# Down projection: the streamed weight pieces issued from ScalarE, and the fourth chain of weight sums in idle gate tiles

## The chip, the cores and the metric

The kernel runs on one core of one Trainium2 chip. The metric is the device time of one execution in microseconds (us). The kernel before takes 1087.72 us, the median of three runs (1086.67 to 1089.07). All data is float32.

## The reference

One block of a network on 512 tokens with 1024 features: a gated convolution branch and a state-space branch, mixed and added to `x`, and then a feed-forward part. The change touches only the last lines of this (with `FFN_HIDDEN` = 2816):

```python
    x = x + rms_norm(mixed, mix_post_g[i])
    h = rms_norm(x, ffn_pre_g[i])
    gt, up = jnp.split(h @ w_gate_up[i], 2, axis=-1)
    f = (jax.nn.silu(gt) * up) @ w_down[i]
    x = x + rms_norm(f, ffn_post_g[i])
```

The product `@ w_down` is the **down projection**: 512 tokens x 2816 features times 2816 x 1024 weights. `h @ w_gate_up` just ahead of it is the **gate/up stage**.

## The kernel before, in words

**Split numbers.** TensorE (PE) multiplies a reduced-precision float32 type. Every operand is therefore kept as two tiles, a high part `hi` (a ScalarE copy that rounds) and a low part `lo` (VectorE: source minus `hi`), and each product is three matmuls, hi x hi, hi x lo and lo x hi (`mm3`, lines 171 to 173). In this text a ScalarE copy is a *cast* and the VectorE subtraction a *sub*.

**The down projection.** Of the 22 blocks of 128 features, 16 go through a Strassen-Winograd scheme. The weights of these 16 blocks are cut into four quarters S11, S12, S21, S22; each quarter is stored as four pieces of 128 x 1024 numbers, 512 KB. Seven products replace eight, and each has four *jobs*, one for each piece j = 0 to 3, so there are 28 jobs of 12 matmuls. This document numbers them in the order in which they run:

| product | jobs | weights of job j | activations |
|---|---|---|---|
| p1 | 0 to 3 | S11 | `f32` as it is |
| p5 | 4 to 7 | S11 + S12 | a difference, made by VectorE |
| p6 | 8 to 11 | S11 + S12 + S22 | two sums, made by VectorE |
| p3 | 12 to 15 | S22 | a difference |
| p7 | 16 to 19 | S12 + S22 | a sum already there |
| p2 | 20 to 23 | S21 | as it is |
| p4 | 24 to 27 | S11 + S12 + S22 + S21 | as it is |

(Signs are put into the activations.) The other six feature blocks follow as plain products, "d".

**The chain.** The weights of p1, p5, p6 and p4 are made in place in one tile for each j, `chain0` to `chain3`. SyncE (SP) reads S11 into it; after the cast and the sub of p1, GpSimd (POOL) issues a DMA that reads S12 and *adds* it to the tile in memory (`chain_add`, line 1074); after those of p5 it adds S22 in the same way; in p2 VectorE adds S21 (line 1093). `chain0` to `chain2` (`NCE` = 3) have tiles of their own, read four steps before the end of the gate/up stage. For `chain3` there is no room then. Its S11 is read twice: once early into a streaming buffer, for job 3 alone (`raw_read("p1", NCE)`), and once into `chain3` in the pool `pf`, which takes the space of the gate/up stage and so can be filled only when that stage has ended (line 1030, called after `h2.close()`).

**The streamed pieces.** The weights of p3, p7 and p2, twelve pieces, pass through five rotating buffers (tag `raw`); each is read by a DMA that SP issues (`raw_read`, line 1069), and for p7 a POOL DMA adds S22 to it (line 1071). The same buffers serve the gate/up weights before and the plain products' weights after. A read waits for the last reader of its buffer, which is the sub of the piece five places earlier.

**Order.** Python code traces the instructions; a scheduler then orders each engine's stream by dependences, buffers and its own estimate of time, so an engine's order is not simply that of the code. Each engine then runs its stream in order, and an instruction whose input isn't there holds up all that stand behind it. `tc.keep_in_program_order(i)` pins `i` behind the instruction traced just before it on the same engine, without waiting for that one's result. `prepare(n)` is called ahead of job n: it traces the forms (activations, `f_form`, lines 1109 to 1122; weights, `w_form`, lines 1087 and 1088) up to job n + `S_AHEAD` = n + 4, and then the reads up to job n + `R_AHEAD` = n + 7.

**The gate tiles.** `second(u)` and `third(u)` of the gate/up stage keep the activated gate of a step in two 128 x 512 tiles, tags `sg0` and `sg1`, two buffers each, in the pool `h2e` (line 982). Only even steps take a new pair; step 20 takes the last. The other pair is last read by `third(19)` (lines 1017 and 1019).

Of the kernel before, what the change touches and what calls it, by code (L numbers as in the profile page):

```python
# [10 lines left out]
F32 = mybir.dt.float32  # L11
# [3 lines left out]
ALU = mybir.AluOpType  # L15
# [3 lines left out]
P = 128  # L19
T = 512  # L20
# [58 lines left out]
NPAIR = 8  # L79
NCE = 3  # L80
NQ = NPAIR // 2
S_AHEAD = 4
R_AHEAD = 7
BLOCKS = ("s11", "s12", "s21", "s22")

TAPS_GLU = 12
# [28 lines left out]
def block_kernel(ctx: ExitStack, tc: tile.TileContext, x, xT, prm, hp, gp, w, out):  # L115
# [863 lines left out]
    fp = ctx.enter_context(tc.tile_pool(name="f", bufs=1, side="right"))  # L979
    f32 = fp.tile([P, NF, T], F32, name="f32")  # L980
    ce = ctx.enter_context(tc.tile_pool(name="ce", bufs=1, side="right"))
    h2e = h2.enter_context(tc.tile_pool(name="h2e", bufs=2, side="right"))
    sg = {}
    c1, c2 = slice(0, HB), slice(HB, T)

# [39 lines left out]
    def piece_of(b, j):  # L1025
        return w[seq[(b, j)]]

    def chain_read(j, pool_):
        chain[j] = pool_.tile([P, 1024], F32, name=f"chain{j}")
        tc.keep_in_program_order(nc.sync.dma_start(chain[j], piece_of("s11", j)))  # L1030

    prev = None
    for u in range(NF):
        if u == NF - 4:
            for j in range(NCE):
                chain_read(j, ce)
        prep_s(u)
        prep_a(u + 1)
        prep_s(u + 1)
        if u >= EARLY_U:  # L1040
            first(u)
        if prev is not None:
            third(u - 1, prev)
        prev = second(u)
# [17 lines left out]

    def raw_read(p, j):
        key = (p, j)
        if key in read or (p in ("p5", "p6", "p4")) or (p == "p1" and j < NCE) or p == "d":
            return
        b = {"p1": "s11", "p3": "s22", "p7": "s12", "p2": "s21"}[p]
        t = read[key] = wp.tile([P, 1024], F32, tag="raw", bufs=RAW_BUFS, name=f"raw_{p}_{j}")
        tc.keep_in_program_order(nc.sync.dma_start(t, piece_of(b, j)))
        if p == "p7":  # L1070
            pool.dma_start(t, piece_of("s22", j), accum_op=ALU.add)

    def chain_add(b, j):
        pool.dma_start(chain[j], piece_of(b, j), accum_op=ALU.add)

    def w_form(n):
        p, j = jobs[n]
        if n in w_forms:
            return
        if p == "d":  # L1080
            w_split(seq[("wd", j)])
            w_forms[n] = split[seq[("wd", j)]]
            return
        raw_read(p, j)
        src = read[p, j] if (p, j) in read else chain[j]
        hi, lo = w_forms[n] = w_room(n)
        act.copy(hi, src)
        dve.tensor_tensor(out=lo, in0=src, in1=hi.bitcast(F32), op=ALU.subtract)
        follow = {"p1": "s12", "p5": "s22"}.get(p)
        if follow and (p, j) not in read:  # L1090
            chain_add(follow, j)
        if p == "p2":
            dve.tensor_tensor(out=chain[j], in0=chain[j], in1=src, op=ALU.add)

    def f_form(n):
        p, j = jobs[n]
# [27 lines left out]
    f_form(0)  # L1124
    for j in range(2):
        w_form(j)
    raw_read("p1", NCE)
    third(NF - 1, h2_last)
    h2.close()
    pf = ctx.enter_context(tc.tile_pool(name="pf", bufs=1))  # L1130
    room["pf"] = pf
    gpost1 = pf.tile([P, D], F32, name="gpost1")
    for j in range(NCE, NQ):
        chain_read(j, pf)
    nc.scalar.dma_start(gpost1, gp[1].partition_broadcast(P))
    room["s"] = pf.tile([P, NPAIR, HB], F32, name="s")
    ev = {(n, r): pf.tile([P, T], F32, name=f"ev{n}{r}") for n in ("p1", "p5", "p6", "mg") for r in range(2)}
    banks = {}

    def acc(name, r):  # L1140
# [16 lines left out]
    for n, (p, j) in enumerate(jobs[: NQ * len(PRODUCTS)]):  # L1157
        if n == 0:
            for m in range(2, NQ):
                w_form(m)  # L1160
            for m in range(NCE, NQ):
                chain_add("s12", m)
        prepare(n)
        name = dict(PRODUCTS)[p]
        (fh, fl), (wh, wl) = f_forms[p, j // 2], w_forms[n]
        for e in range(2):
            c, k = slice(e * T, (e + 1) * T), 2 * (j % 2) + e
            for r in range(2):
                tok = slice(r * P, (r + 1) * P)
                step(name, r, fh[:, k, tok], fl[:, k, tok], wh[:, c], wl[:, c], j == NQ - 1 and e == 1)  # L1170
        if j == NQ - 1:
            for r in range(2):
                if p in ("p1", "p5", "p6"):
                    act.copy(ev[p, r], banks[name, r])
                elif p == "p7":
                    dve.tensor_tensor(out=ev["p5", r], in0=banks[name, r], in1=ev["p5", r], op=ALU.add)
            if p == "p7":
                x2 = f32[:, :NPAIR, :].rearrange("p (t n) d -> p t (n d)", t=NT)
                tc.keep_in_program_order(nc.sync.dma_start(x2, x2d.rearrange("(t p) d -> p t d", p=P)))
# [25 lines left out]
    for t in range(NT):  # L1205
        i, r = t % 2, t // 2
        mg, sq = {}, {}
        for n in (1, 0):
# [2 lines left out]
            b_ = banks[NAME[i, n], r]  # L1211
            if (i, n) == (1, 0):
                sq[n] = mean_sq(b_, pf, f"c{t}", n)
                mg[n] = ev["mg", r]
            else:
                mg[n] = ev[{(0, 0): "p1", (0, 1): "p6", (1, 1): "p5"}[i, n], r]
                dve.tensor_tensor(out=mg[n], in0=b_, in1=mg[n], op=ALU.add if (i, n) == (0, 1) else ALU.subtract)
                sq[n] = mean_sq(mg[n], pf, f"c{t}", n)
                b_ = mg[n]
# [84 lines left out]
```

## Time and profile before

| | us |
|---|---|
| median of three runs | 1087.72 |
| the profiled execution, its own time | 1088.74 |
| its span (first to last instruction) | 1087.0 |
| gate/up stage's last matmul, p1's first matmul at | 960.36 |
| plain products run to about | 1080 |

All times of day in this document are microseconds from the span's start. A timeline row gives start, duration, engine, line, operation, output<-inputs, and in brackets how long the engine stood idle just before and what released it. "PEq", "SPq", "ACTq" are an engine's DMA issues. A row ending in "x2" is two instructions of one kind merged, from the first's start to the last's end. In a table of windows each engine's column is busy time and, in brackets, instructions; PEclk is the clock granted to TensorE, and the DMA share is that of the core's 16 DMA engines. A releaser is inferred: with two candidates the row shows the later one.

### The profile page before, as it was taken

What the parts mean: (1) busy time and instruction counts of PE and PEld (TensorE: products, weight loads), DVE (VectorE), ACT (ScalarE), POOL (GpSimd) and SP (SyncE); (2) the same over time, 40 slices, a digit from 0 to 9 for tenths busy, and PEclk for the clock granted to TensorE, in tenths of its full rate; (3) what the DMA queues carried; (4) which work ended last, traced back from release to release, by engine and by line L of the source; (5) the groups of instructions that cost most, each with busy time, mean ns of one, the idle gap of its engine ahead of it and who ended that gap; (6) DMA issues with size and microseconds to landing.
All of it is one profiled execution on the core that took longest, in us unless ns stands there. A gap on an engine that the chain in (4) does not pass through costs nothing.

```text
span 1087.0 us, 15652 instructions
## 1 busy us (share of the span) xinstructions
PE 1055.5 (97%) x6145; PEld 926.7 (85%) x6145; DVE 827.8 (76%) x1175; ACT 603.4 (56%) x968; POOL 89.3 (8%) x113
## 2 busy tenths in 40 slices
PE   8999999999999999999999999999999999997997
PEld 6888888988897889879888788878999999985886
DVE  6799995996698769697894455579988788658675
ACT  6657848586748464924223762466554554536541
POOL 2002001111111111100000000010000000011000
PEclk9999999999999999999999999999999999998999
DMA  7466643646535553452133222423343243166912
GB/s 280 126 175 208 153 120 98 175 117 194 136 98 142 160 138 102 117 136 78 39 97 117 78 97 78 174 97 117 116 137 98 85 159 126 26 185 147 287 53 78
DMA packets 38954, 139.80 MB, mean 129 GB/s; under 512 B 4576, under 2 KB 4832, under 8 KB 37856
## 3 DMA queue, kind: packets, MB, share of 16 engines
q1 hardware_dynamic: 28896, 99.93, 27.9%
q0 software_dynamic: 7776, 32.51, 14.5%
q10 hardware_dynamic: 2208, 6.36, 1.7%
q8 instruction: 48, 0.79, 0.3%
q14 instruction: 26, 0.21, 0.1%
HBM read 134.52 MB, written 4.26 MB: 128 GB/s over the span
## 4 chain that ended last, share of the span: by engine, by line
PE 76%; DVE 11%; ACT 3%; DMA 3%; issue 2%; POOL 1%; DVEq 0%; POOLq 0%; ACTq 0%; SPq 0%
PE xy L171 4%; PE xy L172 3%; PE xy L173 3%; PE pso L171 3%; PE pso L173 3%; PE pso L172 3%; PE yd L558 2%; PE px L173 2%; PE px L171 2%; PE px L172 2%; PE pz L171 2%; PE pz L172 2%; PE pz L173 2%; DMA raw<-in_w 2%; DVE a L398 2%
## 5 line engine op out<-in xcount | busy, mean ns | idle before, releaser
L138 ACT CAST whi<-raw 128x1024 fp32r<-128x1024 f32 (+1 forms) x118 | 120.8, 1032 | 213.9 <-PE pC L172 37.9
L398 DVE SCALAR_TENSOR_TENSOR a<-v,prm_t,a 128x485 f32<-128x485 f32 (+16 forms) x240 | 182.0, 762 | 4.2 <-ACT a L395 1.4
L143 DVE TENSOR_TENSOR wlo<-raw,whi 128x1024 fp32r<-128x1024 f32 (+1 forms) x84 | 99.7, 1194 | 46.4 <-ACT whi L138 46.3
L171 PE MATMUL pz<-whi,hhi 128*128 128x256 f32 (+1 forms) x256 | 73.6, 287 | 0.8 <-DVE sg L424 0.8
L172 PE MATMUL pz<-wlo,hhi 128*128 128x256 f32 (+1 forms) x256 | 72.2, 282 | 0.0
L173 PE MATMUL pz<-whi,hlo 128*128 128x256 f32 (+1 forms) x256 | 71.9, 281 | 0.0
L829 DVE TENSOR_TENSOR wlo_g<-raw,whi_g 128x1024 fp32r<-128x1024 f32 x40 | 48.2, 1220 | 10.1 <-ACT whi_g L828 10.1
L828 ACT CAST whi_g<-raw 128x1024 fp32r<-128x1024 f32 x40 | 40.9, 1048 | 23.9 <-issue 9.8
L141 POOL DMA_DIRECT2D wlo<-in_w x34 | 30.3, 892 | 274.8 <-ACT wlo L140 163.9
L171 PE MATMUL pso<-yh,whi 128*128 128x512 f32 x128 | 50.5, 396 | 0.6 <-DVE B L475 0.6
L173 PE MATMUL px<-hhi,wlo 128*128 128x512 f32 x128 | 50.4, 394 | 0.0
L172 PE MATMUL px<-hlo,whi 128*128 128x512 f32 x128 | 50.3, 393 | 0.0
L171 PE MATMUL px<-hhi,whi 128*128 128x512 f32 x128 | 50.2, 392 | 0.0
L173 PE MATMUL pso<-yh,wlo 128*128 128x512 f32 x128 | 50.2, 392 | 0.0
L172 PE MATMUL pso<-yl,whi 128*128 128x512 f32 x128 | 50.0, 391 | 0.0
L171 PEld LDWEIGHTS pz<-whi,hhi 128*128 128x128 f32 x256 | 48.3, 189 | 1.3 <-DVE sg L424 1.0
L172 PEld LDWEIGHTS pz<-wlo,hhi 128*128 128x128 f32 x256 | 48.1, 188 | 0.3
L173 PEld LDWEIGHTS pz<-whi,hlo 128*128 128x128 f32 x256 | 48.2, 188 | 0.2
L381 ACT ACTIVATE L<-L,nacs 128x128 f32<-128x128 f32 x128 | 41.4, 392 | 5.8 <-POOL L L375 5.6
L593 DVE TENSOR_SCALAR y<-y,rs 128x256 f32<-128x256 f32 x32 | 9.4, 349 | 36.2 <-POOL rs L179 36.2
L140 ACT ACTIVATE wlo<-whi 128x1024 fp32r<-128x1024 f32 x34 | 35.9, 1055 | 0.2
L475 DVE SCALAR_TENSOR_TENSOR x<-px,prm_t,x 128x511 f32<-128x511 f32 (+2 forms) x48 | 35.3, 743 | 0.5 <-ACT x L473 0.3
(512 smaller groups left out, 3388.7 us busy)
## 6 DMA issues: line engine op xcount, KB each, us to landing
raw<-in_w SPq DMA_DIRECT2D x161, 512.0 KB, 3.7
wlo<-in_w POOLq DMA_DIRECT2D x34, 512.0 KB, 5.3
L<-scr POOLq DMA_DIRECT2D x8, 1024.0 KB, 5.4
raw_p<-in_w SPq DMA_DIRECT2D x13, 512.0 KB, 9.0
chain<-in_w POOLq DMA_DIRECT2D x8, 512.0 KB, 8.5
xT<-in_xT SPq DMA_DIRECT2D x8, 256.0 KB, 5.6
xr<-in_x ACTq DMA_DIRECT2D x4, 512.0 KB, 4.9
x2d<-xr ACTq DMA_DIRECT2D x4, 512.0 KB, 2.6
```

The lines of the kernel that those rows point to most:

```text
L138: act.copy(hi[:, c], src[:, c])
L140: act.activation(lo[:, c], hi[:, c].bitcast(F32), AF.Copy, scale=-1.0)
L141: pool.dma_start(lo[:, c], w[n][:, c].bitcast(F32R), accum_op=ALU.add)
L143: dve.tensor_tensor(out=lo[:, c], in0=src[:, c], in1=hi[:, c].bitcast(F32), op=ALU.subtract)
L171: mark["pe"] = pe.matmul(ps, lh, rh, start=start, stop=False, skip_group_check=more)
L172: pe.matmul(ps, lh, rl, start=False, stop=False, skip_group_check=more)
L173: pe.matmul(ps, ll, rh, start=False, stop=stop, skip_group_check=more)
L381: act.activation(L[:, h, c, :], L[:, h, c, :], AF.Exp, bias=nacs[:, c, HG * g + h : HG * g + h + 1])
L398: return dve.scalar_tensor_tensor(out=va[j][:, d:], in0=vs[j][:, : T - d], scalar=col("dw_w", j * KC + KC - 1 - d), in1=va[j][:, d:], op0= ...
L475: dve.scalar_tensor_tensor(out=a[:, d:], in0=ps[:, : T - d], scalar=col("ssm_w", i * KS + KS - 1 - d), in1=a[:, d:], op0=ALU.mult, op1=ALU ...
L828: a_ = act.copy(hi, src)
L829: d_ = dve.tensor_tensor(out=lo, in0=src, in1=hi.bitcast(F32), op=ALU.subtract)
```

## The change

1. **Streaming reads.** The twelve reads of p3, p7 and p2 are issued by ScalarE (ACT) in place of SP, pinned in program order: each behind the ACT instruction traced just before it. With `R_AHEAD` = 8 that is the cast of job m-4 for the read of job m: the read for job 12 stands behind the cast of job 8, the read for job 16 behind the cast of job 12, and so on.
2. **The fourth place of the chain.** `chain3` is now two 128 x 512 halves in the idle pair of gate tiles, read by SP in the last step of the gate/up stage (`u == NF - 1`). The separate read of S11 for job 3 goes away. Job 3's, 7's, 11's and 27's casts and subs, both POOL additions and p2's VectorE addition are done by halves. The S12 addition to `chain3` now follows job 3's form, as for the other places.
3. **Space.** `h2e` is kept to the end of the kernel; `pf` loses `chain3` and the two `evmg` tiles, for which two idle 128 x 512 slices of `f32` are used.

```diff
-R_AHEAD = 7
+R_AHEAD = 8
...
-    h2e = h2.enter_context(tc.tile_pool(name="h2e", bufs=2, side="right"))
+    h2e = ctx.enter_context(tc.tile_pool(name="h2e", bufs=2, side="right"))
...
-    def chain_read(j, pool_):
-        chain[j] = pool_.tile([P, 1024], F32, name=f"chain{j}")
-        tc.keep_in_program_order(nc.sync.dma_start(chain[j], piece_of("s11", j)))
+    def chain_read(j):
+        if j < NCE:
+            chain[j] = [(ce.tile([P, 1024], F32, name=f"chain{j}"), slice(0, 1024))]
+        else:
+            chain[j] = [
+                (h2e.tile([P, T], F32, tag=f"sg{i}", bufs=2, name=f"chain{j}_{i}"), slice(i * T, (i + 1) * T))
+                for i in range(2)
+            ]
+        for t, c in chain[j]:
+            tc.keep_in_program_order(nc.sync.dma_start(t, piece_of("s11", j)[:, c]))
...
-                chain_read(j, ce)
+                chain_read(j)
+        if u == NF - 1:
+            chain_read(NCE)
...
-        if key in read or (p in ("p5", "p6", "p4")) or (p == "p1" and j < NCE) or p == "d":
+        if key in read or p not in ("p3", "p7", "p2"):
             return
-        b = {"p1": "s11", "p3": "s22", "p7": "s12", "p2": "s21"}[p]
+        b = {"p3": "s22", "p7": "s12", "p2": "s21"}[p]
         t = read[key] = wp.tile([P, 1024], F32, tag="raw", bufs=RAW_BUFS, name=f"raw_{p}_{j}")
-        tc.keep_in_program_order(nc.sync.dma_start(t, piece_of(b, j)))
+        tc.keep_in_program_order(nc.scalar.dma_start(t, piece_of(b, j)))
         if p == "p7":
             pool.dma_start(t, piece_of("s22", j), accum_op=ALU.add)
 
     def chain_add(b, j):
-        pool.dma_start(chain[j], piece_of(b, j), accum_op=ALU.add)
+        for t, c in chain[j]:
+            pool.dma_start(t, piece_of(b, j)[:, c], accum_op=ALU.add)
...
-        src = read[p, j] if (p, j) in read else chain[j]
         hi, lo = w_forms[n] = w_room(n)
-        act.copy(hi, src)
-        dve.tensor_tensor(out=lo, in0=src, in1=hi.bitcast(F32), op=ALU.subtract)
-        follow = {"p1": "s12", "p5": "s22"}.get(p)
-        if follow and (p, j) not in read:
-            chain_add(follow, j)
+        for src, c in [(read[p, j], slice(0, 1024))] if (p, j) in read else chain[j]:
+            act.copy(hi[:, c], src)
+            dve.tensor_tensor(out=lo[:, c], in0=src, in1=hi[:, c].bitcast(F32), op=ALU.subtract)
+        if p in ("p1", "p5"):
+            chain_add({"p1": "s12", "p5": "s22"}[p], j)
         if p == "p2":
-            dve.tensor_tensor(out=chain[j], in0=chain[j], in1=src, op=ALU.add)
+            for t, c in chain[j]:
+                dve.tensor_tensor(out=t, in0=t, in1=read[p, j][:, c], op=ALU.add)
...
-    raw_read("p1", NCE)
...
-    for j in range(NCE, NQ):
-        chain_read(j, pf)
...
-    ev = {(n, r): pf.tile([P, T], F32, name=f"ev{n}{r}") for n in ("p1", "p5", "p6", "mg") for r in range(2)}
+    ev = {(n, r): pf.tile([P, T], F32, name=f"ev{n}{r}") for n in ("p1", "p5", "p6") for r in range(2)}
...
-            for m in range(NCE, NQ):
-                chain_add("s12", m)
...
-                mg[n] = ev["mg", r]
+                mg[n] = f32[:, NPAIR + r, :]
```

## The prediction

> **What bounds the kernel now.** The page first: PE is busy nearly all the span, so only a stage where PE stands still can give much.
>
> ```profile
> span 1087.0 us, 15652 instructions
> PE 1055.5 (97%) x6145; PEld 926.7 (85%) x6145; DVE 827.8 (76%) x1175; ACT 603.4 (56%) x968; POOL 89.3 (8%) x113
> ```
>
> Then the table of windows over the down projection, cut where PE's timeline changes pace:
>
> ```profile
> 961.90:972.80 10.90, 10.90 (x50) 9.02 (x49) 8.93 (x8) 5.56 (x6) 2.86 (x4) 1.00 0.89 266
> 972.80:984.45 11.65, 10.13 (x42) 7.45 (x41) 4.61 (x4) 3.53 (x5) 2.29 (x3) 1.00 1.07 268
> 984.45:990.68 6.23, 0.00 (x1) 0.00 (x0) 3.72 (x5) 4.04 (x5) 0.87 (x1) 0.74 1.05 209
> 990.68:994.41 3.73, 3.69 (x8) 2.48 (x9) 3.73 (x4) 3.73 (x5) 0.00 (x0) 0.52 0.08 14
> ```
>
> PE stands still for 6.23 us, and then runs at a granted clock of 0.52. PE's timeline gives the size of the whole:
>
> ```profile
> 960.36 0.40 PE L171 MATMUL sx<-whi_s,whi_g 128*128 128x512 f32 x1
> ...
> 971.27 0.39 PE L171 MATMUL sv<-phi_s,fh 128*128 128x512 f32 x1
> ...
> 980.36 0.50 PE L171 MATMUL sv<-whi_s,fh 128*128 128x512 f32 x1 [0.76 <-ACT whi_s L1087]
> 981.62 0.50 PE L172 MATMUL sv<-wlo_s,fh 128*128 128x512 f32 x1 [0.76 <-DVE wlo_s L1088]
> ...
> 990.68 0.79 PE L171 MATMUL sx<-whi_s,fh 128*128 128x512 f32 x1 [6.23 <-ACT fh L1118]
> ...
> 994.48 0.40 PE L173 MATMUL sx<-whi_s,fl 128*128 128x512 f32 x1
> ```
>
> p1's 48 matmuls take 971.27 - 960.36 = 10.91 us, 0.2273 each. At that pace p6 (job 8) would start at 960.36 + 96 x 0.2273 = 982.18, and its ninth matmul, the one at 994.48, at 984.00. So the stage has lost **10.48 us** there: 2.1 in p5 (job 7), 6.4 waiting for p6's first activation `fh` (together 8.50), 1.98 to the slow clock after the stand.
>
> Why `fh` is late is in ACT's timeline, whose releasers are the additions to the chain:
>
> ```profile
> 961.83 0.36 ACTq L1135 DMA_DIRECT2D gpost<-in_gp  x1
> ...
> 972.21 1.05 ACT L1087 CAST phi_s<-chain 128x1024 fp32r<-128x1024 f32 x1 [4.26 <-DMA chain<-in_w]
> 979.26 1.05 ACT L1087 CAST whi_s<-chain 128x1024 fp32r<-128x1024 f32 x1 [5.99 <-DMA chain<-in_w]
> ...
> 982.35 1.05 ACT L1087 CAST whi_s<-chain 128x1024 fp32r<-128x1024 f32 x1 [1.07 <-DMA chain<-in_w]
> ...
> 987.69 1.04 ACT L1087 CAST whi_s<-chain 128x1024 fp32r<-128x1024 f32 x1 [1.47 <-DMA chain<-in_w]
> 988.64 1.04 ACT L1087 CAST whi_s<-raw_p 128x1024 fp32r<-128x1024 f32 x1
> 989.58 1.05 ACT L1118 ACTIVATE fh<-s 128x1024 fp32r<-128x1024 f32 x1
> ```
>
> These are the casts of jobs 6, 7, 8, 10 and 12, and then p6's `fh`, which waits for no data of its own at 989.58: it stands in ACT's stream behind job 10's cast, and that waits for S22 being added to `chain2`. POOL's and SP's timelines and the DMA view (960 to 992) tell what these additions wait for:
>
> ```profile
> 961.82 0.86 POOL L1074 DMA_DIRECT2D chain<-in_w  x1 [14.17 <-DVE f L1019]
> 970.39 1.78 POOL L1074 DMA_DIRECT2D chain<-in_w  x2 [7.71 <-DVE wlo_s L1088]
> 972.50 0.86 POOL L1074 DMA_DIRECT2D chain<-in_w  x1 [0.33 <-DMA chain<-in_w]
> 979.49 0.87 POOL L1074 DMA_DIRECT2D chain<-in_w  x1 [6.13 <-DMA chain<-in_w]
> 982.63 0.87 POOL L1074 DMA_DIRECT2D chain<-in_w  x1 [2.28 <-issue]
> ```
> ```profile
> 962.35 57.44 SPq L1069 DMA_DIRECT2D raw_p<-in_w  x12
> ```
> ```profile
> q0 software_dynamic: 1007, 3.67, 57.8%
> q1 hardware_dynamic: 864, 3.15, 26.2%
> q10 hardware_dynamic: 144, 0.52, 6.1%
> ...
> chain<-in_w POOLq DMA_DIRECT2D x6, 512.0 KB, 9.6
> raw_p<-in_w SPq DMA_DIRECT2D x5, 512.0 KB, 12.4
> ...
> chain<-in_w SPq DMA_DIRECT2D x1, 512.0 KB, 7.5
> raw_p<-in_w POOLq DMA_DIRECT2D x1, 512.0 KB, 7.1
> ```
> ```profile
> DMA to landing us min/median/max: 8.8/8.8/8.8
> ```
> ```profile
> DMA to landing us min/median/max: 8.1/8.1/8.1
> ```
>
> The order on POOL is S12 to `chain2`, S12 to `chain3`, S22 to `chain0`, 1, 2, 3. The two landings are those of the issues at 970.39 (979.2) and 979.49 (987.6). The DMA engines are the bound: their share is 0.89, 1.07 and 1.05 in the first three windows. One addition costs them 57.8% of 32 us over 7, **2.64 us**; one read 26.2% over 6, **1.40 us**; the broadcast of `gpost` 1.95 us. From about 963.5 (the first issues stand at 961.8, and 1.7 us to the first bytes is my choice) to the landing that frees `fh` they serve 5 additions, 6 reads and `gpost`: 13.2 + 8.4 + 1.95 = 23.55, so 987.05. The trace has 987.6: the account closes. Five of those six reads are streamed pieces that nobody needs before p3; the sixth is `chain3`'s own S11.
>
> **The change part by part.**
>
> *The reads move behind casts.* The read for job 12 can't leave before job 8's cast, so while the chain is summed the five early reads (7.0 us of DMA) are gone. *`chain3` is read ahead.* Its buffers are the gate tiles that `third(19)` reads last:
>
> ```profile
> 943.68 0.42 DVE L1019 SCALAR_TENSOR_TENSOR f<-xy,sg 128x256 f32<-128x256 f32 x1
> ...
> 960.19 1.22 DVE L1088 TENSOR_TENSOR wlo_s<-chain,whi_s 128x1024 fp32r<-128x1024 f32 x1
> ```
>
> So SP may read at 944.1, and with the 7.5 us of that read in the rows above it lands at 951.6, nine before the sub of job 2, which job 3's form follows. SP is blocked until 944.1, but behind it stands nothing that is needed until the output's residual is loaded. That takes away the last early read, 1.4 us. S12 to `chain3` now waits for job 3's sub instead of the read: job 2's sub ends at 961.4, job 3's two halves about 1.5 later, so POOL issues at about 963 in place of 970.4.
>
> *The new account.* Up to job 10's sum the engines now serve `gpost` and five additions, 15.15 us from 963.5: it lands at **978.7** if nothing else shares the engines, at **981.5** if the reads for jobs 12 and 13 (issued when jobs 8 and 9 have their sums) come in ahead with 2.8 us. From that landing to `fh` the trace has 2.0 us (987.6 to 989.58) and to PE 1.1 more: p6 starts between 981.8 and 984.6, where 982.18 is free of any stand. I take the middle, a rest of **1.0 us** (0 to 2.4); at that length the slow clock should not come, since it doesn't after the two stands of 0.76 (PEclk 1.00 in that window). p5's 2.1 us go, because job 7's sum lands at about 971 and is needed at 979.5.
>
> *What ACT pays.* An issue on ACT is `gpost`'s 0.36 us; twelve make 4.3 us in a stage in which ACT is idle half the time (5.56 and 3.53 busy in the first two windows). Most are made while it would wait for a landing; the one behind job 10's cast can stand ahead of `fh`: **0.3** (0 to 1.1, three issues). Halved casts and subs add a fixed cost of some tenths four times each and lie beside DMA waits: 0.
>
> *What is late next.* The read for job 17 waits for a buffer that job 12's sub frees, and now holds up ACT, with the forms of p3 behind it. p7 has its own addition, so it is the tightest:
>
> ```profile
> 1007.96 0.88 POOL L1071 DMA_DIRECT2D raw_p<-in_w  x1 [1.83 <-DVE wlo_s L1088]
> ...
> 1020.83 1.23 DVE L1088 TENSOR_TENSOR wlo_s<-raw_p,whi_s 128x1024 fp32r<-128x1024 f32 x1 [0.26 <-ACT whi_s L1087]
> ```
>
> That is job 19's piece; its sub ends at 1022.06, and PE takes job 19 at 994.48 + 124 x 0.2273 = 1022.67: 0.6 to spare, and only because the slow clock gave 2.0. Without it, at the same distance from `fh` (1022.06 - 989.58 = 32.5, against 1.1 + 132 x 0.2273 = 31.1 on PE), PE would stand 1.4. One addition more in that group (job 16's, formerly issued at its leisure) makes 4.0 the upper bound; the engines idling after 984 (share 0.08 in the fourth window) make 0 the lower one. I take half of the 1.4, **0.7**.
>
> *Sum:* 10.48 - 1.0 - 0.3 - 0.7 = **8.5 us** gained. On the profiled execution's own time, 1088.74, that is 1080.2; this execution lies 1.0 above the median, so against runs like those shown I say 1087.72 - 8.5 = **1079.2**.
>
> A rule speaks against the change: the Trainium skill, "DMA: Bandwidth & Descriptors", section "Issuing engines are not separate DMA queues", says that DMAs run on the same 16 engines whoever issues them, and that another issuer saves only sequencer time. The account above agrees with it (a share of 1.07 with three issuers at work); what it makes of the time is the second rival.
>
> **The rivals.**
>
> *Half the gain.* The scheduler may put p6's `fh` behind more of ACT's stream: it already stands behind a cast it doesn't need (job 12's at 988.64). If it comes behind job 11's cast, the sixth addition counts too: 981.3 to 984.1, then 2.0 + 1.1: PE from 984.4 to 987.2, a stand of 2.2 to 5.0. Less that, 0.3 and p7's 1.4, the gain is 3.8 to 6.6: 1081.1 to 1083.9, **1082.5** (the slow clock, 2.0 at most, could come on top of the longest stand). Against it: VectorE, which is busy for 4.61 of 11.65 us in the second window, can have `fh`'s source ready early.
>
> *Nothing gained.* If the reads are only moved to another issuer and still leave early, the engines serve the same bytes, less `chain3`'s own read: 1.4 us, **1086.3**. Against it: the pin ties each read to a cast that waits for an addition.
>
> *Slower: ACT's stream jams.* ACT now holds waits for buffers that SP held before (the line of twelve issues lasted 57 us). If the scheduler puts the reads for jobs 16 and 17 and the casts of 12 and 13 ahead of p6's `fh`, as it put job 12's, then `fh` waits for a read that left only after job 8's sum (975), landed 7 to 12 us later by the rows above, was cast and subtracted, and for the next ones. It decides from `fh` at 989.6: each us beyond is one lost. Job 13's piece, read behind job 9's cast at about 978, lands 12 later; a cast, a sub and two issues (1.05 + 1.23 + 0.72) give 993.0, with the slow clock as before: 3.4 slower, **1091**. For it: job 12's place today. Against it: the scheduler would have to expect p6's sums later than p3's pieces.
>
> **How the numbers follow.** The forecast 0.62, half the gain 0.19, nothing 0.07, slower 0.09; 0.03 for a gain beyond the account. The forecast's own bounds are 10.48 less 0 and 10.48 less (2.4 + 1.1 + 1.4): 1077.2 to 1082.1. Reaching to most of the half gain, and with the spread of the three runs at the low end, the range is 1076.6 to 1085.5. About 0.2% (2.2 us) is what a measurement of this kernel can tell from no change: faster 0.84 (the first two and the last), same 0.07, slower 0.09.
>
> **What would show it.** Right: no share near 1 of the DMA engines after 985; S12 added to `chain3` issued by POOL near 963 as two; job 7's cast near 971; p6's first matmul near 983 with a stand under 2.5 us and no slow clock after it; reads as ACT issues from about 975. Wrong: `fh` of p6 behind job 11's cast or later; a stand at jobs 17 to 19 over 2 us; ACT idle with a buffer as releaser while PE stands.

## The result, and the profile after

The changed kernel takes 1080.76 us, the median of six runs (1078.03 to 1083.55), against 1087.79 for the kernel before (six runs, 1086.54 to 1089.07). The ratio is 0.9933, with a 95% interval of 0.9914 to 0.9952: 7.0 us faster. The prediction was 1079.2 (1076.6 to 1085.5). The profiled execution took 1080.67 in place of 1088.74.

The page's first lines after the change (span; busy time, share and instructions of each engine):

```profile
span 1078.9 us, 15644 instructions
PE 1054.5 (98%) x6145; PEld 926.7 (86%) x6145; DVE 827.3 (77%) x1180; ACT 603.9 (56%) x972; POOL 91.3 (8%) x115
```

PE's work is the same; seven to eight microseconds in which it stood still or ran slowly are gone. The waits of PE over the down projection (output, line, what it waited for: total, times, longest) are down to two, and the wait for p6's `fh` is not among them (`fh` and `fl` are the high and the low part of a job's activations, `whi_s` or `phi_s` and `wlo_s` or `plo_s` those of its weights):

```profile
PE sx L172 <- DVE plo_s L1098: 1.8, 1, 1.8
PE sy L172 <- DVE plo_s L1098: 0.4, 1, 0.4
```

PE's timeline shows where they are. The rows are the first matmuls of p1 and p6, and two in job 18:

```profile
959.54 0.40 PE L171 MATMUL sx<-whi_s,whi_g 128*128 128x512 f32 x1
...
981.33 0.39 PE L171 MATMUL sx<-whi_s,fh 128*128 128x512 f32 x1
...
1009.14 0.50 PE L171 MATMUL sx<-phi_s,fh 128*128 128x512 f32 x1
1011.41 0.50 PE L172 MATMUL sx<-plo_s,fh 128*128 128x512 f32 x1 [1.76 <-DVE plo_s L1098]
```

p6 starts 21.79 us after p1, and two products of 10.91 are 21.82: no stand at all, and no slow clock. Reading the first matmul of each product off the same timelines gives a table that the rest of this section and all experiments use (us after p1's first matmul; "lost" is what lies above PE's own pace, 65.46 at p4):

| kernel | p1 at | p5 | p6 | p3 | p7 | p2 | p4 | lost |
|---|---|---|---|---|---|---|---|---|
| PE's own pace | | 10.91 | 21.82 | 32.73 | 43.64 | 54.55 | 65.46 | 0 |
| before | 960.36 | 10.91 | 30.32 | 43.22 | 54.10 | 64.98 | 76.07 | 10.6 |
| after | 959.54 | 10.91 | 21.79 | 32.67 | 43.55 | 57.35 | 68.91 | 3.5 |

Up to p3 the change gains 43.22 - 32.67 = 10.55 us, the whole loss. Then p7 takes 57.35 - 43.55 = 13.80 instead of 10.88, a new loss of 2.92, and p2 loses 0.47 more than before: 10.55 - 2.92 - 0.47 = 7.16. With p1 starting 0.82 earlier that is 7.98 of the 8.07 between the two profiled executions. p1's place is not the change's doing: over the fourteen profiles of this study it lies between 956.94 and 960.65, in code that differs only at its very end. So single profiles are compared from p1 on, and a difference of a few us between single runs says nothing.

**Why p6 is in time.** SP's, POOL's and ACT's timelines of the changed kernel:

```profile
943.01 0.80 SPq L1037 DMA_DIRECT2D chain<-in_w  x2
```
```profile
961.00 1.82 POOL L1084 DMA_DIRECT2D chain<-in_w  x2 [14.17 <-DVE f L1019]
963.66 0.87 POOL L1084 DMA_DIRECT2D chain<-in_w  x1 [0.85 <-DVE wlo_s L1098]
...
992.76 0.89 POOL L1080 DMA_DIRECT2D raw_p<-in_w  x1 [15.11 <-DMA raw_p<-in_w]
...
1003.99 0.86 POOL L1080 DMA_DIRECT2D raw_p<-in_w  x1 [3.08 <-DMA raw_p<-in_w]
```
```profile
970.53 0.62 ACT L1097 CAST whi_s<-chain 128x512 fp32r<-128x512 f32 x1 [0.57 <-DMA chain<-in_w]
...
974.01 1.05 ACT L1097 CAST whi_s<-chain 128x1024 fp32r<-128x1024 f32 x1 [1.88 <-DMA chain<-in_w]
974.02 0.34 ACTq L1078 DMA_DIRECT2D raw_p<-in_w  x1
...
977.48 1.06 ACT L1128 ACTIVATE fh<-s 128x1024 fp32r<-128x1024 f32 x1
979.61 1.05 ACT L1097 CAST whi_s<-chain 128x1024 fp32r<-128x1024 f32 x1 [1.06 <-DMA chain<-in_w]
...
988.07 0.34 ACTq L1078 DMA_DIRECT2D raw_p<-in_w  x1
...
1008.04 1.05 ACT L1097 CAST phi_s<-raw_p 128x1024 fp32r<-128x1024 f32 x1 [2.17 <-DMA raw_p<-in_w]
```

`chain3` is read at 943.01; the last S12 addition leaves at 963.66 (before: 970.39); the second half of job 7 is cast at 970.53 (before: 979.26, in one piece); the first streaming read leaves at 974.02. Job 10's sum, seen by its cast at 979.61, lands inside the 978.7 to 981.5 of the account. But `fh` of p6 now stands ahead of that cast in ACT's stream, at 977.48. The last sum that it stands behind is job 9's (cast at 976.50), and PE needs it only at 981.33.

**Why p7 is late.** p7's first read leaves at 988.07, pinned behind job 12's cast, and its addition follows at 992.76. Before, POOL's rows for the first two of the same four additions were

```profile
985.46 0.87 POOL L1071 DMA_DIRECT2D raw_p<-in_w  x1 [1.95 <-issue]
1003.85 0.87 POOL L1071 DMA_DIRECT2D raw_p<-in_w  x1 [17.52 <-DVE wlo_s L1088]
```

The first addition was issued while PE stood still. Now all four, with their reads, fall into one stretch, and the DMA engines are full again (windows of one product each, p6, p3 and p7's first 10.9 us; and the DMA view of 985 to 1013):

```profile
981.35:992.26 10.91, 10.91 (x50) 9.04 (x49) 10.00 (x10) 7.75 (x10) 0.00 (x0) 1.00 0.71 218
992.26:1003.20 10.94, 10.94 (x50) 9.07 (x49) 6.09 (x6) 4.51 (x6) 2.62 (x3) 1.00 0.96 233
1003.20:1014.10 10.90, 8.98 (x38) 6.50 (x36) 6.98 (x6) 5.28 (x6) 0.86 (x1) 1.00 1.03 298
```
```profile
q10 hardware_dynamic: 1161, 4.21, 45.7%
q0 software_dynamic: 577, 2.10, 39.0%
...
raw_p<-in_w ACTq DMA_DIRECT2D x9, 512.0 KB, 6.2
raw_p<-in_w POOLq DMA_DIRECT2D x4, 512.0 KB, 7.9
```

45.7% of 28 us, over the 4.21 MB that the reads moved, is 1.59 us for each 512 KB (eight pieces; the ninth, issued at 1011.94, had hardly begun); 39.0% over four additions is 2.73. Both are a little above the prices that the prediction took from another stretch (1.40 and 2.64). Job 18's sum therefore lands only just ahead of its cast at 1008.04, and VectorE, in order, does two other things before its sub:

```profile
1007.86 1.22 DVE L1103 TENSOR_TENSOR chain<-chain,raw_p 128x1024 f32<-128x1024 f32 x1 [1.70 <-DMA raw_p<-in_w]
1009.00 1.22 DVE L1132 SCALAR_TENSOR_TENSOR fl<-f,fh 128x1024 fp32r<-128x1024 f32 x1
1010.14 1.22 DVE L1098 TENSOR_TENSOR plo_s<-raw_p,phi_s 128x1024 fp32r<-128x1024 f32 x1
```

VectorE waits 1.70 us for a piece of p2, which job 18 doesn't need. Whether the late data or this order costs PE its wait is one of the questions below.

### The profile page after: what moved, and what is told of

It is laid out like the page before. It is cut to its first block, busy times and chain, and to the rows that moved or that the text cites. A ratio compares the mean times of both kernels' runs of the same rounds, so it can differ in the third digit from the quotient of the medians.

```text
span 1078.9 us, 15644 instructions
## 1 busy us (share of the span) xinstructions
PE 1054.5 (98%) x6145; PEld 926.7 (86%) x6145; DVE 827.3 (77%) x1180; ACT 603.9 (56%) x972; POOL 91.3 (8%) x115
## 4 chain that ended last, share of the span: by engine, by line
PE 66%; issue 11%; DVE 9%; ACT 6%; DMA 3%; POOL 2%; POOLq 0%; DVEq 0%; ACTq 0%
PE xy L171 3%; PE xy L172 3%; PE xy L173 3%; PE pso L171 3%; PE pso L173 3%; PE pso L172 3%; PE yd L558 2%; DVE a L398 2%; DMA chain<-in_w 1%; PE px L173 1%; PE px L172 1%; PE pgs L171 1%; DMA raw_p<-in_w 1%; PE pgs L173 1%; PE px L171 1%
```

## The experiments

The theory was that of the prediction: the DMA engines, loaded with early reads, made p6 late; both parts together empty them. The rivals were that one part alone does it, that ACT's order (`fh` behind casts it doesn't need) does it, and that ScalarE as issuer matters for itself. Each kernel is timed against the kernel before on the same chip; the ratios can be compared with the change's 0.9933. "Places" are those of the table above, for their profiles:

| kernel | p5 | p6 | p3 | p7 | p2 | p4 | lost |
|---|---|---|---|---|---|---|---|
| chain_ahead_only | 10.94 | 21.82 | 38.66 | 49.55 | 60.43 | 71.31 | 5.9 |
| act_reads_only | 10.96 | 22.64 | 37.94 | 48.82 | 63.79 | 75.36 | 9.9 |
| sp_reads_held | 10.94 | 24.43 | 38.63 | 49.51 | 60.39 | 71.27 | 5.8 |
| before_fh_first | 10.91 | 26.92 | 42.37 | 53.25 | 64.13 | 75.02 | 9.6 |
| before_fh_both | 10.93 | 27.05 | 42.30 | 53.17 | 64.05 | 74.93 | 9.5 |
| chain_ahead_fh | 10.92 | 21.80 | 32.78 | 43.66 | 55.00 | 66.75 | 1.3 |
| ahead9 | 10.96 | 21.84 | 33.34 | 44.22 | 60.86 | 71.74 | 6.3 |
| adds_later | 10.95 | 21.83 | 32.71 | 43.59 | 57.93 | 70.59 | 5.1 |
| p7_from_p3 | 10.96 | 21.84 | 33.02 | 43.90 | 55.86 | 66.98 | 1.5 |
| p7_from_p3_sp | 10.96 | 23.02 | 34.86 | 45.74 | 56.62 | 67.50 | 2.0 |
| p7_from_p3_adds_later | 10.95 | 21.83 | 32.76 | 43.64 | 54.52 | 65.66 | 0.2 |
| p7_from_p3_sp_fh | 10.95 | 21.83 | 32.71 | 43.59 | 54.47 | 65.35 | 0 |

### Each part alone

**chain_ahead_only**: the change without its first part; SP issues the reads (`R_AHEAD` stays 8).

```diff
-        tc.keep_in_program_order(nc.scalar.dma_start(t, piece_of(b, j)))
+        tc.keep_in_program_order(nc.sync.dma_start(t, piece_of(b, j)))
```

> Part 2 of the change alone: chain3 by halves in the gate tiles, read ahead; the twelve streaming reads stay on SP. Theory 1 (time of the transfers): SP no longer stands until 961 behind chain3's read, so the five reads that have a free buffer leave at about 943 to 946, while the DMA engines are three tenths busy, and are served before the additions begin at 961. Then only gpost and five additions lie ahead of p6, as in the change: p6 starts without a stand at about 981 to 982. Job 16's piece is read and summed early again and ScalarE is not held up by buffers, so p7 stands less than the 2.7 us of the change: 1077 to 1080 us, equal to the change or up to 3 us faster. Theory 2 (the issuer): it is the issue from ScalarE behind the casts that takes the reads out of the additions' way; without it they are back: 1085 to 1088 us.

**act_reads_only**: the kernel before with the first part alone; p1's own streamed read stays on SP.

```diff
-R_AHEAD = 7
+R_AHEAD = 8
...
-        tc.keep_in_program_order(nc.sync.dma_start(t, piece_of(b, j)))
+        eng = nc.sync if p == "p1" else nc.scalar
+        tc.keep_in_program_order(eng.dma_start(t, piece_of(b, j)))
```

> Part 1 of the change alone: p3's, p7's and p2's reads on ScalarE behind the casts; chain3 as before (S11 for job 3 through a streaming buffer on SP, chain3 read when the gate/up stage has ended). Theory 1: chain3's read (1.4 us of the engines) and its later S12 addition lie ahead of p6, and the addition waits for that read (issue about 967 in place of 963): p6 starts 1.5 to 4 us late, p7 as in the change: 1081 to 1084.5 us. Theory 2: nearly the whole gain, 1080 to 1081.5 us.

Measured: the chain's part alone takes 1080.01 us (1079.16 to 1082.81; ratio 0.993 [0.9916, 0.9945]), as good as the whole change. The issuer's part alone takes 1086.13 (1083.85 to 1092.29; ratio 0.9983 [0.9969, 0.9997]), a gain of 2 us and less than expected.

Why the first is enough is in SP's timeline of chain_ahead_only, and in its window ahead of p1, beside that of the changed kernel and, last, the kernel before (the last two columns are the DMA share and GB/s):

```profile
943.62 67.47 SPq L1078 DMA_DIRECT2D raw_p<-in_w  x12
```
```profile
944.00:959.29 15.29, 15.29 (x129) 15.29 (x129) 4.63 (x10) 4.24 (x9) 1.80 (x2) 1.00 0.94 265
```
```profile
944.00:959.54 15.54, 15.54 (x131) 15.54 (x131) 4.87 (x10) 4.35 (x9) 1.80 (x2) 1.00 0.49 102
```
```profile
944.00:960.36 16.36, 16.36 (x138) 16.36 (x137) 5.70 (x11) 4.41 (x10) 1.80 (x2) 1.00 0.36 65
```

In the kernel before, SP's stream was held by `chain3`'s one read until the gate/up stage had ended, and five reads that need nothing left behind it, at 962.35, into the busiest stretch. With that read gone they leave at 943.62, into fifteen microseconds in which the DMA engines were two thirds idle. So there are two ways to empty the stretch of the chain: later reads (the change) or earlier ones. The prediction saw only the first. No run reads `chain3` ahead and leaves the five reads at their old time, so what each of the two brings is not separated.

chain_ahead_only still loses 5.9, all in p6: not at its start but at its second half, whose `fh` stands in ACT's stream behind job 10's late cast and the casts of p3's early pieces:

```profile
982.59 1.05 ACT L1097 CAST whi_s<-chain 128x1024 fp32r<-128x1024 f32 x1 [4.40 <-DMA chain<-in_w]
...
986.61 1.04 ACT L1097 CAST phi_s<-raw_p 128x1024 fp32r<-128x1024 f32 x1
987.55 1.05 ACT L1128 ACTIVATE fh<-s 128x1024 fp32r<-128x1024 f32 x1
```

Job 10's cast is late because job 16's piece, read early too, is summed ahead of it. POOL's timeline:

```profile
970.04 0.86 POOL L1080 DMA_DIRECT2D raw_p<-in_w  x1
973.88 0.87 POOL L1084 DMA_DIRECT2D chain<-in_w  x1 [2.98 <-DVE f L1121]
```

The second row is S22 to `chain2`, 14.59 us after p1's first matmul; in the changed kernel it leaves at 12.07 (971.61). It seems to wait for one of three places: in these traces the later additions of the chain leave 0.2 to 0.3 us after the third one before them has landed (here at 973.88 after job 8's sum, cast at 973.65; in the changed kernel at 974.24 after 974.01; in the kernel before at 979.49 after 979.26). This is read off the rows, and no run tests it. The prediction's account has no term for it.

act_reads_only shows what the first part brings and costs. It takes p6's start from 30.32 to 22.64, but p6 itself then takes 15.30, and p7 takes 14.97. In p6 the sums are late, since `chain3`'s own S11 is still read late: its S12 addition leaves 9.93 us after p1's first matmul, in the changed kernel 4.12, and job 10's cast comes at 25.52 in place of 20.07. PE's longest wait there, 1.80, is for the first `fl`, which stands behind other work of VectorE, so late sums are not all of it. Both large losses at p7, here and in the changed kernel, come with the reads on ACT. No kernel with the reads on SP loses more than 0.5 us there; most of these reach p7 later, but chain_ahead_fh (below) reaches it at 43.66, like the change, and loses 0.46.

### The issuer with the same order in time

**sp_reads_held**: the change, but SP issues the reads, each held by a copy of 256 bytes from the cast behind which the change pins it. (Twelve small transfers are added.)

```diff
+    held, mark_d = [None], dr2.tile([16, 64], F32, name="mark_d")
...
+        tc.keep_in_program_order(nc.sync.dma_start(mark_d[len(read) : len(read) + 1, :], held[0][:1, :64].bitcast(F32)))
         t = read[key] = wp.tile([P, 1024], F32, tag="raw", bufs=RAW_BUFS, name=f"raw_{p}_{j}")
-        tc.keep_in_program_order(nc.scalar.dma_start(t, piece_of(b, j)))
+        tc.keep_in_program_order(nc.sync.dma_start(t, piece_of(b, j)))
...
         hi, lo = w_forms[n] = w_room(n)
+        held[0] = hi
```

> The change, but with the twelve reads on SP, each held until the same cast by a 256-byte copy of that cast's result to memory, issued on SP just ahead of the read. Same times of the reads, another issuer. Theory 1: as the change, within 1.5 us (1078.5 to 1082), since the time at which the transfers leave is what counts. Theory 2: the gain is lost or halved, 1084 to 1088 us.

Measured: 1082.60 us (1081.72 to 1087.03; ratio 0.9953 [0.9936, 0.997]). ACT's timeline, PE's, and windows from the end of the wait on:

```profile
980.81 0.62 ACT L1100 CAST phi_s<-chain 128x512 fp32r<-128x512 f32 x1 [2.12 <-DMA chain<-in_w]
981.33 1.05 ACT L1131 ACTIVATE fh<-s 128x1024 fp32r<-128x1024 f32 x1
```
```profile
982.43 0.79 PE L171 MATMUL sx<-whi_s,fh 128*128 128x512 f32 x1 [2.46 <-ACT fh L1131]
```
```profile
982.00:988.80 6.80, 6.32 (x14) 4.58 (x15) 5.53 (x6) 5.32 (x8) 0.00 (x0) 0.50 0.71 251
988.80:990.80 2.00, 2.00 (x10) 1.63 (x10) 2.00 (x3) 1.82 (x3) 0.89 (x1) 1.00 0.02 4
```

This is the rival "half the gain" of the prediction, in another kernel: `fh` behind the first half of job 11's cast, a stand of 2.46. The reads are tied to the same casts, and the sums are no later: job 10's cast comes 19.64 us after p1's first matmul, in the changed kernel 20.07. What differs in the traces at p6 is ACT's order, since in the changed kernel `fh` comes ahead of job 10's cast. No term of the sum contained a new place for `fh` in the scheduler's order. The issuer alone does not set that place: chain_ahead_only, with SP, has `fh` ahead of job 10's cast too, and p7_from_p3_sp (below), also with SP, has it where it is here. After the short stand PE also ran at a clock of 0.50 for 6.8 us, which the prediction had not expected after so short a stand; more on that at the end. The time falls between the expectation's two ranges, and its interval overlaps the change's, so by time alone the issuer makes no difference that these runs show.

### ACT's order alone

**before_fh_first** holds the casts of jobs 10 and 12 behind p6's first `fh` in the kernel before; **before_fh_both** holds those of jobs 10 and 11 behind its first and those of 12 to 15 behind its second; **chain_ahead_fh** does the latter in chain_ahead_only. `not_before(a, b)` puts `a` behind `b` in an engine's order without a wait for data, and `mark` keeps the instruction that it refers to. The edit of the last two (in before_fh_both without the `[:, c]`):

```diff
-            act.copy(hi[:, c], src)
+            cast = act.copy(hi[:, c], src)
+            if 10 <= n < 16:
+                not_before(cast, mark["fh", "p6", n // 12])
...
-        act.activation(hi, src, AF.Copy, scale=sign)
+        mark["fh", p, q] = act.activation(hi, src, AF.Copy, scale=sign)
```

> The kernel before, with one thing changed: p6's first activation is put ahead of the casts of jobs 10 and 12 in ScalarE's order, where it needs to wait for nothing that lands after 985.2. Transfers as before. Theory 1 (the DMA engines' load is the cause): p6 starts at 986.5 to 988 instead of 990.7, but its second half then waits for the sums that still land at 987 to 991; 0 to 4 us gained, 1084 to 1088 us. Rival (ScalarE's order is the cause): more than half of the change's gain, 1080 to 1083.5 us.

> The kernel before with ScalarE's order alone changed: p6's first activation before the casts of jobs 10 to 11, its second before those of jobs 12 to 15. Transfers as before. Theory 1a (load and order both): p6 still starts 4 to 5 us late, since job 8's and 9's sums land at 982 and 985, and its second half no longer waits behind casts: 3 to 5.5 us gained, 1082.5 to 1085 us. Theory 1b (load alone): 0 to 2 us, 1085.5 to 1088 us. Order alone: 1080 to 1082 us.

> Part 2 of the change alone (reads on SP), and p6's two activations put ahead in ScalarE's order: the first before the casts of jobs 10 and 11, the second before those of jobs 12 to 15. Theory 1a (load of the DMA engines, and on top of it the place of p6's activations in ScalarE's order; ScalarE's issue gains by setting that order): p6's loss of 6.0 us in the profile of part 2 alone falls to 0 to 2, and p7 has none: 1075.5 to 1078.5 us. Theory 1b (only the load; the addition for job 16 that got in among the chain's is the whole rest): p6 keeps 3 us or more of its loss: 1078.5 to 1081 us.

Measured: before_fh_first 1086.13 us (1084.48 to 1087.65; ratio 0.9987 [0.9977, 0.9997]), before_fh_both 1085.96 (1085.09 to 1088.0; 0.999 [0.9981, 0.9998]), chain_ahead_fh 1079.72 (1076.84 to 1082.10; 0.9926 [0.9911, 0.9941]).

Order by itself is worth some 1.3 us. In before_fh_both `fh` is early, and PE starts p6 3.3 us sooner than before, but then it lacks the next things, and the clock falls at the same price:

```profile
PE sx L171 <- ACT fh L1120: 2.9, 1, 2.9
PE sx L173 <- DVE fl L1122: 1.6, 1, 1.6
...
```
```profile
986.10:992.85 6.75, 5.16 (x12) 3.53 (x12) 6.75 (x8) 5.16 (x7) 0.00 (x0) 0.51 0.51 100
```

So the bound of the kernel before was the data, as the prediction had it, and not the place of `fh` behind the casts of jobs 10 and 12. (In both runs `fh` still stands behind job 9's cast, at 983.81 in before_fh_both, and no run puts it further ahead.) chain_ahead_fh loses 1.3 in its profile against 5.9 without the edit; the two medians, 1079.72 and 1080.01, don't tell the two apart. A profile is one execution, and chain_ahead_only's was the slowest of its six. So the profile bears out the first theory of the expectation (order on top of load), and the time, 1079.72, does not: it lies in the range of the second.

### Where p7's loss comes from

**ahead9**: the change with each read one cast earlier (`R_AHEAD` = 9). **adds_later**: the change with p2's chain additions on VectorE held behind job 19's sub.

```diff
-R_AHEAD = 8
+R_AHEAD = 9
```
```diff
+            mark["sub", n] = dve.tensor_tensor(out=lo[:, c], in0=src, in1=hi[:, c].bitcast(F32), op=ALU.subtract)
...
-                dve.tensor_tensor(out=t, in0=t, in1=read[p, j][:, c], op=ALU.add)
+                not_before(dve.tensor_tensor(out=t, in0=t, in1=read[p, j][:, c], op=ALU.add), mark["sub", 5 * NQ - 1])
```

> The change with R_AHEAD = 9: every read on ScalarE stands one cast earlier, so job 16's piece is read behind job 11's cast (985) and not job 12's (988). Theory 1: p7's four additions form a queue that is bound by the DMA engines from 993 on; the first starts 2 to 3 us earlier, and p7's stand of 2.7 falls to 0 to 1.5; job 12's piece read behind job 7's cast puts 1.4 us ahead of job 10's sum, for which p6 has about 3 us to spare: 1078 to 1080.5 us. Rival (the reads for jobs 17 to 19, which wait for buffers in either version, set the stand): 1080 to 1082 us.

> The change, with p2's additions to the chain on VectorE held behind the sub of job 19 in VectorE's own order. In the profile of the change, job 18's sub starts 1.1 us after its cast is done, because an addition to the chain and an activation that was held up behind it stand ahead. If VectorE's order is the cause of p7's stand: 1.1 us or more less, 1078.5 to 1080 us. If late data is (the piece landed at 1008.0, 1.5 us after it was needed): at most 1.1 us less and the rest stays, 1079.5 to 1081.5 us.

Both expectations failed. ahead9 takes 1084.33 us (1082.03 to 1087.84; ratio 0.9973 [0.9962, 0.9984]), slower than the change. adds_later takes 1082.18 (1080.32 to 1083.90; 0.9953 [0.9937, 0.9969]), no better than it.

In ahead9 job 16's read is earlier (25.90 us after p1's first matmul, in the change 28.53), but those of jobs 17 and 18 are not (31.34 and 33.61, in the change 30.71 and 32.98). ACT's timeline has two later ones, waiting for buffers, in front of p7's `fh` and of further casts; VectorE's has two chain additions for p2 ahead of job 18's sub, and the second waits for data:

```profile
995.00 1.47 ACTq L1078 DMA_DIRECT2D raw_p<-in_w  x2
```
```profile
1010.16 1.22 DVE L1103 TENSOR_TENSOR chain<-chain,raw_p 128x1024 f32<-128x1024 f32 x1 [1.55 <-DMA raw_p<-in_w]
1011.30 1.22 DVE L1098 TENSOR_TENSOR plo_s<-raw_p,phi_s 128x1024 fp32r<-128x1024 f32 x1
```

p7 takes 16.64, a wait of 3.1 and then half a clock again. This is a mild form of the rival "ACT's stream jams". In adds_later VectorE is free, and waits itself, for the cast of a sum that lands late:

```profile
1009.49 1.05 ACT L1097 CAST phi_s<-raw_p 128x1024 fp32r<-128x1024 f32 x1 [2.27 <-DMA raw_p<-in_w]
```

p7 takes 14.34, no less than the change's 13.80, and p2 12.66. PE's wait in job 18 does fall, from 1.76 to 0.76, but it then waits 0.76 in job 19 and 1.49 at p2's first job. So with late data VectorE's order is not what binds.

**p7_from_p3** removes the load instead. p7's weights are S12 + S22, and p3's are S22, already in a buffer: after p3's form POOL adds S12 there. p7's four reads go away (2 MB, 5.6 us of the DMA engines), and the four additions no longer wait for a read.

```diff
-        b = {"p3": "s22", "p7": "s12", "p2": "s21"}[p]
+        if p == "p7":
+            read[key] = read["p3", j]
+            pool.dma_start(read[key], piece_of("s12", j), accum_op=ALU.add)
+            return
+        b = {"p3": "s22", "p2": "s21"}[p]
...
-        if p == "p7":
-            pool.dma_start(t, piece_of("s22", j), accum_op=ALU.add)
```

**p7_from_p3_sp** is the same with SP as issuer, **p7_from_p3_sp_fh** adds the two holds on p6's `fh` to that, **p7_from_p3_adds_later** adds to p7_from_p3 the hold on VectorE.

> The change, but p7's weights are made in p3's buffers: after p3's form the POOL DMA adds S12 to the S22 that is already there, so p7's four reads (5.6 us of the engines) go, and each addition can be issued when p3's sub of that piece is done (990 to 996 in place of 993 to 1004). Theory 1 (p7's stand in the change is late data): job 18's and 19's pieces land 6 us or more earlier, no stand in p7: 3 us faster than the change, 1076.5 to 1078.5 us. Rival (the stand comes from the order of VectorE's stream, where an addition to the chain and an activation stand ahead of job 18's sub, both behind the landing of p2's first piece): 1079 to 1081 us.

> p7's weights made in p3's buffers as in the run before, and the eight reads that are left (p3, p2) issued by SP instead of ScalarE. With chain3 read ahead SP isn't blocked, so the first five leave at about 943, and no addition for p7 can get between those of the chain, as one did in the run of the second part alone. Theory 1 (only when the transfers run counts): all stands go: 1076 to 1078 us, equal to the run with ScalarE's issue or up to 1.5 us faster. Theory 2 (ScalarE's issue is what keeps the chain clear): p6 stands again, 1079 to 1083 us.

> p7's weights made in p3's buffers, the other reads on SP, and p6's activations put ahead in ScalarE's order as in the run above. No addition for p7 can get among the chain's, no cast stands ahead of p6's activations: from p1's first matmul to p4's first 65.5 to 66.5 us (65.46 is PE's own time), against 67.5 without the order: 1075.5 to 1077.5 us. If ScalarE's order isn't what p6 waits for in that run: as before, 1078 to 1080 us.

> p7's weights made in p3's buffers with ScalarE's issue, and p2's additions to the chain held behind the sub of job 19 on VectorE. In the profile without that, VectorE stood 3.3 us in front of such an addition while job 18's piece was cast, and p7 lost 1.1. Theory (with the data early, VectorE's order is all that is left of p7's stand): 0.5 to 1.3 us less, 1076 to 1077.3 us. Rival (the additions, now later, are late for p4): 1077.5 to 1080 us.

Measured: p7_from_p3 1077.46 us (1075.84 to 1080.78; ratio 0.9904 [0.9886, 0.9921]), p7_from_p3_sp 1079.56 (1078.24 to 1082.20; 0.9933 [0.9917, 0.9948]), p7_from_p3_sp_fh 1078.14 (1074.78 to 1078.84; 0.9909 [0.9896, 0.9923]), p7_from_p3_adds_later 1078.66 (1075.87 to 1079.34; 0.9913 [0.9901, 0.9925]).

p7_from_p3_sp keeps p7 whole but loses at p6, where `fh` again stands behind half of job 11's cast (PE waits 1.0 for it and 0.5 for `fl`); the holds of p7_from_p3_sp_fh remove that. The chain was clear in p7_from_p3_sp (job 10's cast 20.16 us after p1's first matmul, in the change 20.07), so it does not take the issue from ScalarE to keep it clear. Less load is what p7 needed: in p7_from_p3 it takes 11.96, a loss of 1.1 where the change lost 2.9. What is left there is VectorE's order, which waits for p2's piece ahead of job 18's sub:

```profile
1005.67 1.23 DVE L1105 TENSOR_TENSOR chain<-chain,raw_p 128x1024 f32<-128x1024 f32 x1 [3.30 <-DMA raw_p<-in_w]
...
1007.95 1.22 DVE L1100 TENSOR_TENSOR plo_s<-raw_p,phi_s 128x1024 fp32r<-128x1024 f32 x1
```

Now that the data is early, the hold on VectorE takes this wait away in the profile: p7_from_p3_adds_later loses 0.2 in the whole stage, and p7_from_p3_sp_fh nothing (its windows of p6 and p7, PE busy from end to end):

```profile
978.77:989.65 10.88, 10.88 (x49) 9.01 (x48) 10.26 (x11) 8.37 (x11) 1.76 (x2) 1.00 0.19 26
...
1000.53:1011.41 10.88, 10.88 (x49) 9.01 (x48) 8.69 (x8) 9.28 (x10) 0.00 (x0) 1.00 1.00 368
```

p7_from_p3 beats both kernels by its median, the kernel before by 10.9 us on the same chip. Against the change its interval overlaps a little (0.9886 to 0.9921 against 0.9914 to 0.9952). The best three, 1077.46 to 1078.66, are not told apart, although their profiles lose 1.5, 0 and 0.2 us: what is left of the stage is smaller than the spread of the runs. By time the holds bring nothing that shows, and both kernels with a hold took longer than their theories had said (at most 1077.5 and 1077.3).

## Why the prediction was right, and where its steps were off

**The bound of the kernel before: right.** Five early reads and `chain3`'s second read of S11 kept the DMA engines full while the chain was summed. Taking these bytes out of the stretch, to either side, gives nearly all of the gain (0.993 and 0.9933); ACT's order alone gives a tenth of a per cent.

**The account of the DMA engines: right in its sum.** Job 10's sum landed where the account put it. The prices are not fixed: the DMA view of the changed kernel from 960 to 985 gives 2.98 us for each 512 KB added and 1.24 for each read (its `gpost` taken as 1.95), that of 985 to 1013 gives 2.73 and 1.59, where the account had 2.64 and 1.40.

**The rest stand at p6, 1.0 us: it was 0.** The step took `fh` to stay behind job 10's cast, as in the kernel before. The scheduler put it ahead. That is a gift of the order, and so luck: with job 10's sum at 979.61 and the step's own 2.0 and 1.1 us, p6 would have started at 982.7, a stand of 1.4 (an estimate from these rows), much as the step had it. With `fh` behind the first half of job 11's cast, sp_reads_held stood 2.46 us and lost 3.3 more to the clock.

**ACT's issues, 0.3 us: 0 by the stage.** The changed kernel reaches p3 0.06 us ahead of PE's own pace. The row of 974.02 above begins 0.01 after the start of the cast to which it is pinned (974.01); the issue runs beside the cast.

**What is late next, 0.7 us (0 to 4.0): the term that was mis-sized.** It measured 2.92 in p7 and 0.47 in p2, 3.39 in all, inside its bounds and near the upper one. The step halved a loss of 1.4 because the DMA engines had been idle after 984. But the change itself filled that time: one more sum, formerly at 985.46, and the reads that used to be made earlier. The step named that addition, as its upper bound, and should have started from it. The forecast's own bounds, 1077.2 to 1082.1, were added up with at most 1.4 for this term, not with the 4.0 that the step had named, and so did not allow for what it came to. The sum with the measured terms: 10.55 - 0 - 0 - 3.39 = 7.16, against the forecast 8.5; the runs say 7.0. Two terms that were too large by 1.3 together hid half of the 2.7 by which this one was too small, and that too is luck.

**The rivals.** *Half the gain* did not happen here, and its wait did in sp_reads_held, at 1082.60 where the rival had 1082.5. That the times agree is luck: the rival's middle had 3.6 us of standing and 1.7 for ACT's issues and p7, the run shows 2.6, then 3.3 of slow clock, and no loss at p7. *Nothing gained* failed: the pins do hold the reads back (974.02 and later). As for the rule behind it, from the Trainium skill, "DMA: Bandwidth & Descriptors", "Issuing engines are not separate DMA queues": that another issuer saves only sequencer time agrees with chain_ahead_only, where SP as issuer does as well as ScalarE. What decided was not who issues but what else stands in that engine's stream, and so when the read leaves. *Slower* did not happen; ahead9 shows its beginnings, at 3.6 us more than the change by the medians.

**What was to be seen.** Job 7's cast near 971, the reads from about 975 and `chain3`'s S12 near 963 came as said; p6 came earlier than said, 981.33 against 983. That no share would be near 1 after 985 was wrong: 0.96 and 1.03 during p3 and p7. The list's own sign of an error, a stand over 2 us at jobs 17 to 19, is just missed by the wait itself, 1.76, and is met by what p7 loses, 2.92.

It stays open which share of the gain is `chain3`'s read and which the five reads, and whether the three places for additions bind beside the load of the DMA engines. Nor does any experiment separate how much of the change's p7 loss is the reads and how much the additions, since p7_from_p3 takes away both the reads and the wait for them.

## What to carry to other kernels

Ask first what holds a queue: a read that waits for space holds back all that stand behind it, and moving that one read let five others go 19 us earlier. The two together were worth as much as the whole change (0.993 and 0.9933); moving the twelve reads to another engine was worth 2 us by itself. When a change frees a stretch, look at what it pushes into the next one, and take the bound that contains it as the estimate. An edit that touches one engine's order moves other instructions on it, so check in the trace where the needed ones now stand; and if one part of a summed operand is already on the chip, adding to it saves a read (p7 took 11.96 us in place of 13.80).

## What the runs showed of the hardware that was not expected

The prediction let a stand of up to 2.4 us go without a slow clock. In the down projection six kernels show the granted clock at half after stands of 1.94 to 6.23 us, and what it costs does not follow the length of the stand. Windows cut where the clock changes, for the kernel before and, below it, for chain_ahead_only (its stand 1.94 and 0.53) and ahead9 (3.12):

```profile
987.40:994.10 6.70, 3.38 (x7) 2.27 (x8) 4.64 (x6) 6.41 (x7) 0.00 (x0) 0.50 0.55 109
```
```profile
989.20:996.10 6.90, 6.37 (x16) 4.83 (x16) 6.90 (x8) 4.16 (x5) 0.00 (x0) 0.51 0.30 93
```
```profile
1013.30:1016.60 3.30, 3.30 (x10) 2.53 (x9) 3.30 (x4) 3.30 (x4) 0.00 (x0) 0.50 1.02 412
```

The half clock lasted 6.7 to 6.9 us in five kernels and 3.3 in one. PE loses half of the time that it works in it: 3.38 / 2 = 1.7 in the kernel before, whose long stand used up the rest of the slow time, but 6.32 / 2 = 3.2 in sp_reads_held after 2.46 us of standing. So a short stand can cost more in clock than a long one, and a stand of two to three us came to a loss of five to six (5.9 in sp_reads_held and chain_ahead_only, 5.8 at p7 in ahead9). There was no drop in the changed kernel (1.76), in p7_from_p3_sp (1.02 and 0.53) or in act_reads_only (0.64 and 1.80). The Trainium skill, "TensorE: Matmul & The Clock Gate", "Part 1: The HAM clock gate", puts the drop after an idle window of about 3.4 us, and says that the windows run freely. The lengths of 3.3 and 6.7 to 6.9 agree with one and two such windows; drops after less than 3.4 us of standing don't agree with the first figure, and no run here shows why two kernels with nearly the same stand (1.94 and 0.53, 0.64 and 1.80) differ.
